# Feed forward of a decoder layer: down projection by token with seven quadrant products in place of eight

## The chip, the cores and the metric

One core of one Trainium2 chip. The metric is the time on the device of one execution, in microseconds (us), and lower is better. The engines are TensorE (PE; its weight loads are listed as PEld), VectorE (DVE), ScalarE (ACT), GpSimd (POOL) and SyncE (SP, which issues the kernel's loads). L12 means line 12 of the kernel before.

## What is computed

A decoder layer on 512 tokens of 1024 features in float32. The part around the change:

```
h   = layer_norm(alpha * h + mixed @ w_out, ln1_g, ln1_b)
mlp = square(relu(h @ w_up)) @ w_down        # 1024 -> 4096 -> 1024
r   = alpha * h + mlp
ple = sigmoid(r @ ple_gate_w) * (p @ ple_proj_w)
h   = layer_norm(r + ple, ln2_g, ln2_b)
```

Ahead of it stand an input norm, a combined input projection, a gated delta rule, a pooling mixer and their merge; these the change leaves as they are.

## The kernel before

Wide products run as three passes in float32r over a split of both operands into a high part with 12 significant bits and the rest: high times high, high times low, low times high (`three`, L65). A weight slab of 512 KB is loaded by SP into one of three raw buffers, copied by ACT into the high part and subtracted by DVE into the low part (`load`, L50 to L59; four buffers each for high and low). The activations `act` are kept by feature: [feature, token], in eight blocks of 128 features, each with a high and a low half (L47).

The work goes in stages: the mixers, the output projection `ps_wo` with the norm LN1 (`out_done`, L790), the projection `ps_pp` of p, and from L824 on the feed forward, the gate product and LN2. LN1 normalises 128 tokens at a time in place in `y`, transposes them on PE and writes them to `act` with gain and offset (`to_features`, L109).

The feed forward runs twice over half of the 4096 hidden features (`fh`, L836). Each half makes 8 up slabs of 256 features; per block of 128 features PE runs 24 matmuls of 128x512 (weights held still, tokens moving), ACT takes relu and square (L846, L848), DVE squares again and subtracts for the low part (L849, L850). The 16 blocks of hidden activations stay in the buffers `hid`. Then come the 8 output blocks of the down projection, 96 matmuls each (L860), in two banks at a time; the first half adds alpha times `act` and stores to `rp` (L865, L867), the second adds `rp` (L870), splits into `act` (L871, L872), transposes with four small matmuls per block (L875) and copies back to `rp` (L876), so that r is there by feature for the gate and by token for the residual.

The gate product (`tok_gemm`, L745, called at L918) holds tokens still and moves weights: first 512 columns for all four token blocks with the features outermost, then the other 512 columns block by block, the last in two pieces. `ple_done` (L880) applies the sigmoid on ACT, multiplies by `pproj` on DVE (L886) and adds `rp`, on POOL for the first 512 columns and on DVE for the rest (L887); with the last columns of a block come the statistics and LN2, shared out to DVE, ACT and POOL by `plan` (L895), and the output is stored.

Nothing of the order is written out by hand here: a scheduler places instructions by their order in the program, priorities (`tc.high_priority`) and simulated times; `tc.issue_after` puts instructions behind another one on its engine. Each engine and each queue then runs its list in order. PSUM has eight banks of [128, 512]: six of tag `g` and two of tag `tp` in this stage.

## Time and profile before

| | |
|---|---|
| time, median of 3 runs | 887.84 us (886.15 to 889.31) |
| the profiled execution | span 886.5 us; no other time is listed for it |
| granted clock of PE, mean | 0.990 |
| up and down projections, first up matmul to last down matmul | 476.5 to 829 us |
| first down matmul | 564.7 us |
| last matmul of the gate product | starts at 873.63 us |
| HBM | 77.74 MB read, 90 GB/s over the span |

Busy time is per engine, from the start to the end of each instruction. PE's matmuls overlap: the duration of one is not the distance to the next. "Idle before" is an engine's idle time ahead of a group, followed by what ended it; it costs something only where the engine is the one that sets the time. The DMA row names the issuing queue, the number of issues, the size and the median time from issue to landing. The rows that matter are shown in the prediction.

### The profile page before, as it was taken

What the parts mean: (1) busy time and instruction counts of PE and PEld (TensorE: products, weight loads), DVE (VectorE), ACT (ScalarE), POOL (GpSimd) and SP (SyncE); (2) the same over time, 40 slices, a digit from 0 to 9 for tenths busy, and PEclk for the clock granted to TensorE, in tenths of its full rate; (3) what the DMA queues carried; (4) which work ended last, traced back from release to release, by engine and by line L of the source; (5) the groups of instructions that cost most, each with busy time, mean ns of one, the idle gap of its engine ahead of it and who ended that gap; (6) DMA issues with size and microseconds to landing.
All of it is one profiled execution on the core that took longest, in us unless ns stands there. A gap on an engine that the chain in (4) does not pass through costs nothing.

```text
span 886.5 us, 12477 instructions
## 1 busy us (share of the span) xinstructions
PE 860.3 (97%) x4944; PEld 715.3 (81%) x4944; DVE 521.7 (59%) x991; ACT 357.5 (40%) x567; POOL 151.6 (17%) x135
## 2 busy tenths in 40 slices
PE   7999999999999999998999999999999999999994
PEld 5777888888888888886888888888888888888883
DVE  8898988769759336368366544433344443333456
ACT  4566455365544535333136444322124442222311
POOL 6182312113403031324000000000000000000034
PEclk9999999999999999999999999999999999999997
DMA  6322222222211313183215333333323323233202
GB/s 196 96 59 85 72 73 80 65 72 72 78 50 53 97 31 97 52 283 96 72 32 182 96 95 95 119 96 95 95 85 103 99 95 96 95 96 95 95 10 86
DMA packets 72427, 80.63 MB, mean 91 GB/s; under 512 B 4009, under 2 KB 64818, under 8 KB 72370
## 3 DMA queue, kind: packets, MB, share of 16 engines
q1 hardware_dynamic: 72370, 79.85, 29.6%
q8 instruction: 39, 0.64, 0.3%
q14 instruction: 18, 0.15, 0.1%
HBM read 77.74 MB, written 2.10 MB: 90 GB/s over the span
## 4 chain that ended last, share of the span: by engine, by line
PE 89%; DVE 6%; ACT 2%; POOL 1%; issue 1%; DMA 1%; SPq 0%; POOLq 0%; ACTq 0%; DVEq 0%
PE ps_dn L67 7%; PE ps_dn L68 7%; PE ps_dn L66 7%; PE ps_up L67 6%; PE ps_up L68 6%; PE ps_up L66 6%; PE ps_z L67 2%; PE ps_z L68 2%; PE ps_gb L66 2%; PE ps_gb L68 2%; PE ps_v L67 2%; PE ps_z L66 2%; PE ps_gb L67 2%; PE ps_v L68 2%; PE ps_v L66 2%; PE ps_ga L66 2%
## 5 line engine op out<-in xcount | busy, mean ns | idle before, releaser
L67 PE MATMUL ps_dn<-hid,hi_dn 128*128 128x512 f32 x256 | 99.9, 390 | 0.0
L68 PE MATMUL ps_dn<-hid,lo_dn 128*128 128x512 f32 x256 | 99.9, 390 | 0.0
L66 PE MATMUL ps_dn<-hid,hi_dn 128*128 128x512 f32 x256 | 99.7, 389 | 0.0
L58 DVE TENSOR_TENSOR lo_dn<-raw_dn,hi_dn 128x1024 fp32r<-128x1024 f32 x32 | 39.2, 1225 | 82.9 <-ACT hi_dn L57 82.9
L57 ACT CAST hi_dn<-raw_dn 128x1024 fp32r<-128x1024 f32 x32 | 33.7, 1054 | 96.8 <-PE ps_dn L67 85.2
L887 POOL TENSOR_TENSOR y<-y,rp 128x512 f32<-128x512 f32 x4 | 6.3, 1613 | 380.5 <-PE ps_pg L756 380.5
L66 PEld LDWEIGHTS ps_dn<-hid,hi_dn 128*128 128x128 f32 x256 | 48.1, 188 | 10.0
L67 PEld LDWEIGHTS ps_dn<-hid,hi_dn 128*128 128x128 f32 x256 | 48.1, 188 | 10.0
L68 PEld LDWEIGHTS ps_dn<-hid,lo_dn 128*128 128x128 f32 x256 | 48.1, 188 | 9.7
L849 DVE TENSOR_TENSOR relu<-relu 128x512 f32<-128x512 f32 x32 | 22.2, 693 | 53.3 <-ACT hid L848 53.3
L846 ACT ACTIVATE relu<-ps_up 128x512 f32<-128x512 f32 x32 | 19.0, 595 | 55.8 <-PE ps_up L68 55.8
L693 POOL TENSOR_TENSOR zs<-zs,sgb 128x512 f32<-128x512 f32 x8 | 15.0, 1875 | 88.0 <-ACT sgb L692 88.0
L850 DVE TENSOR_TENSOR hid<-relu,hid 128x512 fp32r<-128x512 f32 x32 | 22.1, 691 | 1.1
L352 DVE SCALAR_TENSOR_TENSOR acc_q<-ps_q,ccol,acc_q 128x511 f32<-128x511 f32 (+2 forms) x24 | 17.8, 742 | 6.3 <-ACT acc_q L350 6.0
L848 ACT ACTIVATE hid<-relu 128x512 fp32r<-128x512 f32 x32 | 20.3, 633 | 1.0
L451 DVE TENSOR_TENSOR sh<-sh,ya 128x120 f32<-128x120 f32 (+14 forms) x60 | 19.4, 324 | 0.7
L356 POOL TENSOR_TENSOR kq<-acc_k,sg_k 128x512 f32<-128x512 f32 x8 | 10.9, 1366 | 48.9 <-ACT sg_k L355 48.9
L58 DVE TENSOR_TENSOR lo_pg<-raw_pg,hi_pg 128x1024 fp32r<-128x1024 f32 x8 | 9.6, 1222 | 16.3 <-ACT hi_pg L57 16.3
L121 ACT ACTIVATE hf_l<-ps_l,pcol 128x128 f32<-128x128 f32 x32 | 11.9, 472 | 17.1 <-PE ps_l L116 17.1
L557 ACT ACTIVATE vn<-ps_s,cc 128x128 f32<-128x128 f32 x32 | 11.1, 367 | 18.6 <-PE ps_s L555 18.5
L352 DVE SCALAR_TENSOR_TENSOR acc_k<-ps_k,ccol,acc_k 128x511 f32<-128x511 f32 (+2 forms) x24 | 17.8, 742 | 1.3 <-ACT acc_k L350 1.2
L58 DVE TENSOR_TENSOR lo_wo<-raw_wo,hi_wo 128x1024 fp32r<-128x1024 f32 x8 | 10.8, 1354 | 13.0 <-ACT hi_wo L57 13.0
(947 smaller groups left out, 2557.0 us busy)
## 6 DMA issues: line engine op xcount, KB each, us to landing
raw_dn<-in_w_down_dram SPq DMA_DIRECT2D x32, 512.0 KB, 3.5
raw_wo<-in_w_out_dram SPq DMA_DIRECT2D x8, 512.0 KB, 4.0
raw_pg<-in_ple_gate_w_dram SPq DMA_DIRECT2D x8, 512.0 KB, 3.6
x<-in_x_dram SPq DMA_DIRECT2D x8, 256.0 KB, 5.3
y<-in_x_dram SPq DMA_DIRECT2D x4, 512.0 KB, 9.3
out_dram<-y SPq DMA_DIRECT2D x7, 256.0 KB, 2.0
raw_k<-in_w_in_dram SPq DMA_DIRECT2D x2, 512.0 KB, 4.0
raw_pp<-in_ple_proj_w_dram SPq DMA_DIRECT2D x2, 512.0 KB
```

Of the source, the lines that this page charges most:

```text
L57: A.copy(hi, raw)
L58: V.tensor_tensor(out=lo, in0=raw, in1=hi.bitcast(F32), op=SUB)
L66: T.matmul(ps, wh, ah, start=first, stop=False)
L67: T.matmul(ps, wh, al, start=False, stop=False)
L68: T.matmul(ps, wl, ah, start=False, stop=last)
L352: marks[name + "v"] = V.scalar_tensor_tensor(out=acc[:, s:], in0=ps[:, :SEQ - s], scalar=w(3 - s), in1=acc[:, s:], op0=MULT, op1=ADD)
L451: V.tensor_tensor(out=sh[:, :, :m], in0=sh[:, :, :m], in1=ya[:, :, k:k + 1].to_broadcast([P, U8, m]), op=MULT)
L693: G.tensor_tensor(out=zs[m], in0=zs[m], in1=sg, op=MULT)
L846: A.activation(r, ps, AF.Relu)
L848: A.activation(hl[:, 0, :], r, AF.Square)
L849: V.tensor_tensor(out=r, in0=r, in1=r, op=MULT)
L850: V.tensor_tensor(out=hl[:, 1, :], in0=r, in1=hl[:, 0, :].bitcast(F32), op=SUB)
```

## The change

The down projection is computed by token, [token, feature], in eight chunks `c` of 512 hidden features, and each chunk's product is made by Strassen's scheme (in Winograd's form). The activations are cut into two halves of tokens (rows) and, within each block of 256 features `j`, two blocks of 128 features (the inner halves); `w_down` into the matching inner halves and two halves of 512 columns. Seven products take the place of eight.

- The left operands are made on DVE. After relu and square (both on ACT now, into `r2`), the quarters a11 (`ha`) and a12, a22 (`hb`) are split for products 1, 2 and 4; four subtractions of [128, 256] make the sums in place in `r2`, and these are split into `hs` for products 6, 7, 3 and 5.
- The right operands are sums of weight quarters, made by DMA. SP loads four quarters of 512 KB a chunk into buffers of their own (`dx`, six). POOL adds other quarters onto them with accumulating DMAs, two of 256 KB per quarter: one sum onto `y`, and three in turn onto `x`. Between the sums on `x` its value is split (`halves`) for the next product: 1, then 5, then 6, then 4. The split parts have buffers of their own (`dhi`, `dlo`, four each).
- The results. Products 1 and 6 gather in four banks of their own over all chunks (`perm`, tag `u`). Products 2, 5 and 7 go into the banks of tag `g` (now four) and are added by DVE to the residual `res` in each chunk (`gather`); products 3 and 4 are made on top of 5 and 7 in the same banks and added too. In the last chunk the standing banks are added as well.
- The residual is kept by token: LN1 writes its normalised rows to `res` in a pool of its own, and in the first chunk DVE applies LN1's gain and offset to it, times alpha, with eight operations of [128, 1024].
- r is transposed for the gate by `features`, per block of 128 tokens. The gate product goes by tokens: all 1024 columns of a block, then the next. DVE makes all additions; POOL none. All eight gate slabs are loaded and split ahead, four of them into `dhi` and `dlo`.
- The up slabs of later chunks have a smaller priority offset (40 in place of 300) and are put behind the splits of the chunk before.

The core of the diff (the feed forward before, removed as a whole, is in the listing above):

```diff
-    def load(src, c, name, keep=None, tags=("whi", "wlo"), nb=4):
...
-        with tc.high_priority(offset=300):
+        with tc.high_priority(offset=ahead):
...
+    rsp = root.enter_context(tc.tile_pool(name="rsp", bufs=1, side="right"))
...
+    res = [rsp.tile([P, DM], F32, name=f"res_{t}") for t in range(NT)]
...
-            V.tensor_scalar(out=y, in0=y, scalar1=mv[:, 0:1], scalar2=rstd, op0=SUB, op1=MULT)
-            to_features(y, t, g_1, b_1, pp2, ("tp",), 2, tpa, "l1")
+            V.tensor_scalar(out=res[t], in0=y, scalar1=mv[:, 0:1], scalar2=rstd, op0=SUB, op1=MULT)
+            to_features(res[t], t, g_1, b_1, pp2, ("tp",), 2, tpa, "l1")
...
+    def g3(name):
+        return pp3.tile([P, SEQ], F32, tag="g", bufs=4, name=name)
+    perm = {i: [pp3.tile([P, SEQ], F32, tag="u", bufs=4, name=f"ps_dn{i}_{m}") for m in range(2)]
+            for i in (1, 6)}
+    NC = 8
+    DXB = 6
+    gb1 = tp3.tile([P, 2, DM], F32, tag="hs", bufs=2, name="gb1")
+    dma(out=gb1[:, 0, :], in_=ln1_g[0].partition_broadcast(P))
+    dma(out=gb1[:, 1, :], in_=ln1_b[0].partition_broadcast(P))
+    def quarter(c, i, half):
+        src = w_down[0, 512 * c:512 * c + 512, 512 * half:512 * half + 512]
+        return src.rearrange("(j i p) n -> i p j n", i=2, p=P)[i]
+    def chain(c, name, i, half):
+        raw = tp3.tile([P, 2, 512], F32, tag="dx", bufs=DXB, name=f"{name}_{c}")
+        dma(out=raw, in_=quarter(c, i, half))
+        return raw
+    def onto_chain(raw, c, i, half):
+        for j in range(2):
+            G.dma_start(out=raw[:, j, :], in_=quarter(c, i, half)[:, j, :], accum_op=ADD)
+    def halves(raw, name):
+        hi = tp3.tile([P, 2, 512], F32R, tag="dhi", bufs=4, name=f"hi_{name}")
+        lo = tp3.tile([P, 2, 512], F32R, tag="dlo", bufs=4, name=f"lo_{name}")
+        marks["dn"] = (A.copy(hi, raw), V.tensor_tensor(out=lo, in0=raw, in1=hi.bitcast(F32), op=SUB))
+        return hi, lo
+    def hidden(c):
+        left = []
+        for j in range(2):
+            c0 = 512 * c + 256 * j
+            with ExitStack() as queue:
+                for ins in behind[j]:
+                    queue.enter_context(tc.issue_after(ins.ins))
+                gr = [slab(w_up[0], k0, c0, f"up{c}{j}{k0}", ahead=40 if c else 300) for k0 in (0, 512)]
+            r2 = tp3.tile([P, 2, SEQ], F32, tag="r2", bufs=2, name=f"r2_{c}{j}")
+            ha = tp3.tile([P, 2, HT], F32R, tag="ha", bufs=2, name=f"hid_a{c}{j}")
+            hb = tp3.tile([P, 2, SEQ], F32R, tag="hb", bufs=2, name=f"hid_b{c}{j}")
+            hs = tp3.tile([P, 2, 2, SEQ], F32R, tag="hs", bufs=2, name=f"hid_s{c}{j}")
+            for i in range(2):
+                ps = g3(f"ps_up{c}{j}{i}")
+                gemm_tile(ps, gr, i, HALVES if c == 0 and j == 0 else ((0, SEQ),))
+                A.activation(r2[:, i, :], ps, AF.Relu)
+                A.activation(r2[:, i, :], r2[:, i, :], AF.Square)
+                src, dst = (r2[:, 1, :], hb) if i else (r2[:, 0, 0:HT], ha)
+                A.copy(dst[:, 0, :], src)
+                V.tensor_tensor(out=dst[:, 1, :], in0=src, in1=dst[:, 0, :].bitcast(F32), op=SUB)
+            a11, a21, a12, a22 = r2[:, 0, 0:HT], r2[:, 0, HT:], r2[:, 1, 0:HT], r2[:, 1, HT:]
+            V.tensor_tensor(out=a22, in0=a21, in1=a22, op=SUB)
+            V.tensor_tensor(out=a21, in0=a11, in1=a21, op=SUB)
+            V.tensor_tensor(out=a11, in0=a11, in1=a22, op=SUB)
+            V.tensor_tensor(out=a12, in0=a12, in1=a11, op=SUB)
+            for k in (1, 0):
+                act_last = A.copy(hs[:, 0, k, :], r2[:, k, :])
+                vec_last = V.tensor_tensor(out=hs[:, 1, k, :], in0=r2[:, k, :], in1=hs[:, 0, k, :].bitcast(F32),
+                                           op=SUB)
+            at = {1: (lambda q, h=ha: h[:, q, :]), 2: (lambda q, h=hb: h[:, q, 0:HT]),
+                  4: (lambda q, h=hb: h[:, q, HT:])}
+            for k, i in enumerate((6, 7, 3, 5)):
+                at[i] = lambda q, h=hs[:, :, k // 2, HT * (k % 2):HT * (k % 2) + HT]: h[:, q, :]
+            left.append(at)
+        behind[0] = (act_last, vec_last)
+        return left
+    def product(i, left, right, banks, first, last, pairs=(0, 1), onto=False):
+        hi, lo = right
+        for j in pairs:
+            for m in range(2):
+                ms = slice(m * P, (m + 1) * P)
+                ah, al = left[j][i](0)[:, ms], left[j][i](1)[:, ms]
+                f, l = first and j == 0, last and j == 1
+                T.matmul(banks[m], ah, hi[:, j, :], start=f, stop=False, skip_group_check=onto)
+                T.matmul(banks[m], ah, lo[:, j, :], start=False, stop=False, skip_group_check=onto)
+                done = T.matmul(banks[m], al, hi[:, j, :], start=False, stop=l, skip_group_check=onto)
+        return done
+    behind = [(), ()]
+    def gather(banks, row, half, op=ADD):
+        for m in range(2):
+            dst = res[2 * row + m][:, 512 * half:512 * half + 512]
+            if op == ADD:
+                V.tensor_tensor(out=dst, in0=banks[m], in1=dst, op=ADD)
+            else:
+                V.tensor_tensor(out=dst, in0=dst, in1=banks[m], op=SUB)
+    def features(t):
+        for half in range(2):
+            ps = pp3.tile([P, 4, P], F32, tag="u", bufs=4, name=f"ps_rt{t}{half}")
+            for a in range(4):
+                kb = 4 * half + a
+                T.transpose(ps[:, a, :], res[t][:, kb * P:(kb + 1) * P], ident)
+            ks, ts = slice(4 * half, 4 * half + 4), slice(t * P, (t + 1) * P)
+            A.copy(act[:, ks, 0, ts], ps)
+            V.tensor_tensor(out=act[:, ks, 1, ts], in0=ps, in1=act[:, ks, 0, ts].bitcast(F32), op=SUB)
+    def start_chains(c):
+        x, z, y = chain(c, "x", 0, 0), chain(c, "z", 1, 0), chain(c, "y", 0, 1)
+        onto_chain(y, c, 1, 1)
+        return x, z, y, chain(c, "w", 1, 1)
+    chains = start_chains(0)
+    for c in range(NC):
+        fst, lst = c == 0, c == NC - 1
+        x, z, y, b22 = chains
+        w = {1: halves(x, f"dn{c}_1")}
+        onto_chain(x, c, 0, 1)
+        w[2] = halves(z, f"dn{c}_2")
+        w[5] = halves(x, f"dn{c}_5")
+        onto_chain(x, c, 1, 1)
+        left = hidden(c)
+        w[6] = halves(x, f"dn{c}_6")
+        onto_chain(x, c, 1, 0)
+        if fst:
+            for t in range(NT):
+                V.scalar_tensor_tensor(out=res[t], in0=res[t], scalar=ALPHA, in1=gb1[:, 0, :], op0=MULT, op1=MULT)
+                V.scalar_tensor_tensor(out=res[t], in0=gb1[:, 1, :], scalar=ALPHA, in1=res[t], op0=MULT, op1=ADD)
+        if not lst:
+            chains = start_chains(c + 1)
+        zb = [g3(f"ps_dnz_{c}{m}") for m in range(2)]
+        xb = [g3(f"ps_dnx_{c}{m}") for m in range(2)]
+        yb = [g3(f"ps_dny_{c}{m}") for m in range(2)]
+        p1 = lambda pairs: product(1, left, w[1], perm[1], fst, lst, pairs)
+        p2 = lambda pairs: product(2, left, w[2], zb, True, True, pairs)
+        p5 = lambda: product(5, left, w[5], xb, True, True)
+        p6 = lambda: product(6, left, w[6], perm[6], fst, lst)
+        p7 = lambda: product(7, left, w[7], yb, True, True)
+        if not lst:
+            p1((0,)), p2((0,)), p1((1,)), p2((1,))
+            gather(zb, 0, 0)
+            w[7] = halves(y, f"dn{c}_7")
+            p5()
+            gather(xb, 1, 1)
+            w[3] = halves(b22, f"dn{c}_3")
+            behind[1] = marks["dn"]
+            p6()
+            w[4] = halves(x, f"dn{c}_4")
+            p7()
+            gather(yb, 1, 1, SUB)
+            product(3, left, w[3], xb, False, True, onto=True)
+            gather(xb, 0, 1)
+            product(4, left, w[4], yb, False, True, onto=True)
+            gather(yb, 1, 0)
+            continue
+        p1((0,)), p2((0,)), p1((1,)), p2((1,))
+        gather(zb, 0, 0)
+        w[3] = halves(b22, f"dn{c}_3")
+        p5()
+        gather(perm[1], 0, 0)
+        gather(xb, 1, 1)
+        w[7] = halves(y, f"dn{c}_7")
+        us, u2 = [], tp3.tile([P, 2, SEQ], F32, tag="r2", bufs=2, name="u")
+        for m in range(2):
+            A.copy(u2[:, m, :], perm[1][m])
+            us.append(u2[:, m, :])
+        p6()
+        for m in range(2):
+            V.tensor_tensor(out=us[m], in0=perm[6][m], in1=us[m], op=SUB)
+        gather(us, 0, 1)
+        w[4] = halves(x, f"dn{c}_4")
+        product(3, left, w[3], xb, False, True, onto=True)
+        gather(xb, 0, 1)
+        p7()
+        features(0)
+        gather(us, 1, 1)
+        gather(yb, 1, 1, SUB)
+        features(1)
+        product(4, left, w[4], yb, False, True, onto=True)
+        gather(us, 1, 0, SUB)
+        gather(yb, 1, 0)
+    features(2)
+    features(3)
...
+    gates = []
+    for half in range(2):
+        kw = dict(keep=tp3, tags=("dhi", "dlo")) if half else {}
+        gates.append([rslab(ple_gate_w[0], 256 * i, 512 * half, f"pg{half}{i}", **kw) for i in range(4)])
+    for t in range(NT):
+        cuts = (0, 512, 1024) if t < NT - 1 else (0, 512, 768, 1024)
+        st = tp3.tile([P, 3, 6], F32, tag="st", bufs=2, name=f"st_l2{t}")
+        for n, (c0, c1) in enumerate(zip(cuts, cuts[1:])):
+            half, w0, w1 = c0 // 512, c0 % 512, (c1 - 1) % 512 + 1
+            ps = pp3.tile([P, SEQ], F32, tag="g", bufs=4, name=f"ps_pg{t}{n}")[:, 0:c1 - c0]
+            for kb in range(KB):
+                hi, lo = gates[half][kb // 2]
+                ah, al = (act[:, kb, q, t * P:(t + 1) * P] for q in range(2))
+                T.matmul(ps, ah, hi[:, kb % 2, w0:w1], start=kb == 0, stop=False)
+                T.matmul(ps, ah, lo[:, kb % 2, w0:w1], start=False, stop=False)
+                T.matmul(ps, al, hi[:, kb % 2, w0:w1], start=False, stop=kb == KB - 1)
+            sg = tp3.tile([P, SEQ], F32, tag="r2", bufs=2, name=f"sg_{t}{n}")[:, 0:c1 - c0]
+            A.activation(sg, ps, AF.Sigmoid)
+            V.tensor_tensor(out=sg, in0=sg, in1=pproj[t, half][:, w0:w1], op=MULT)
+            y = res[t][:, c0:c1]
+            V.tensor_tensor(out=y, in0=y, in1=sg, op=ADD)
+            V.bn_stats(out=st[:, n, :], in_=y)
...
+        plan = (((0, 512, "V"), (512, 1024, "G")), ((0, 512, "V"), (512, 1024, "G")),
...
```

79 lines of the change are left out of this document (10 added, 69 removed).

## The prediction

> **What bounds the kernel now.** I read the page's head first, then busy time by stretches, then single matmuls in order of time, and last who waits for whom.
>
> ```profile
> span 886.5 us, 12477 instructions
> PE 860.3 (97%) x4944; PEld 715.3 (81%) x4944; DVE 521.7 (59%) x991; ACT 357.5 (40%) x567; POOL 151.6 (17%) x135
> ```
>
> ```profile
> 476.00:831.00 355.00, 354.66 (x1625) 295.52 (x1624) 145.63 (x165) 117.99 (x153) 0.00 (x0) 1.00 0.33 100
> 831.00:874.00 43.00, 42.91 (x216) 36.33 (x214) 25.95 (x36) 9.64 (x15) 12.22 (x10) 1.00 0.11 39
> 874.00:887.00 13.00, 0.00 (x0) 0.00 (x0) 7.86 (x14) 1.59 (x3) 6.18 (x6) 0.57 0.21 81
> ```
>
> The columns of the stretches are: length; busy time of PE, PEld, DVE, ACT and POOL; granted clock; DMA share; GB/s. The first row is the feed forward (up and down), the second the rest of the gate product, the third the tail. PE is busy in 354.66 of 355.00 us at clock 1.00, while DVE is busy in 41% and ACT in 33% of it, and POOL does nothing. So in the stage that changes, time is the number of matmuls times their spacing. The spacing is not the duration that the groups show:
>
> ```profile
> 599.82 0.39 PE L67 MATMUL ps_dn<-hid,hi_dn 128*128 128x512 f32 x1
> ...
> 603.90 0.39 PE L67 MATMUL ps_dn<-hid,hi_dn 128*128 128x512 f32 x1
> ```
>
> Columns: start, duration, instruction. A matmul of 128x512 lasts 0.39 us, but they start much closer: from 599.82 to 603.90 there are 18 steps, so the pitch is 4.08 / 18 = 0.2267 us. Whoever multiplied by the 0.39 would see a gain 1.7 times too big.
>
> The tail is a second bound: the last matmul starts at 873.63 and the span ends 12.9 us later.
>
> **The matmuls.** Before, the down projection has 3 x 256 = 768 matmuls (256 for each of L66, L67, L68, group below). After, each of 8 chunks of 512 hidden features makes seven products; each is 2 feature pairs x 2 blocks of 128 tokens x 3 passes = 12 matmuls of 128x512. That is 8 x 84 = 672, so 96 fewer. The up projection keeps its count; the 32 transposes of r stay 32; the gate product keeps its matmuls too. The three passes now hold tokens still and move weights, as the output projection and the gate product already do; loads per matmul stay at one. Gain: 96 x 0.2267 = **21.8 us**. A chunk then takes (96 + 84) x 0.2267 = 40.8 us on PE: 21.8 for up, 19.0 for the products.
>
> **DVE and ACT per chunk.**
>
> ```profile
> L67 PE MATMUL ps_dn<-hid,hi_dn 128*128 128x512 f32 x256 | 99.9, 390 | 0.0
> L58 DVE TENSOR_TENSOR lo_dn<-raw_dn,hi_dn 128x1024 fp32r<-128x1024 f32 x32 | 39.2, 1225 | 82.9 <-ACT hi_dn L57 82.9
> L57 ACT CAST hi_dn<-raw_dn 128x1024 fp32r<-128x1024 f32 x32 | 33.7, 1054 | 96.8 <-PE ps_dn L67 85.2 <-PE ps_up L67 11.6
> L848 ACT ACTIVATE hid<-relu 128x512 fp32r<-128x512 f32 x32 | 20.3, 633 | 1.0
> L846 ACT ACTIVATE relu<-ps_up 128x512 f32<-128x512 f32 x32 | 19.0, 595 | 55.8 <-PE ps_up L68 55.8
> L870 DVE TENSOR_TENSOR rp<-ps_dn,rp 128x512 f32<-128x512 f32 x8 | 5.5, 690 | 3.8 <-PE ps_dn L68 3.8
> L871 ACT CAST act<-rp 128x512 fp32r<-128x512 f32 x8 | 4.9, 618 | 9.9 <-DVE rp L870 9.9
> L703 DVE TENSOR_TENSOR lo_lift<-raw_lift,hi_lift 128x256 fp32r<-128x256 f32 x2 | 0.8, 416 | 0.0
> ```
>
> DVE: 11 weight splits (4 up, 7 down) x 1.225 = 13.5; per block of 256 features 5 half-width subtractions x 0.416 and 3 full ones x 0.69 = 4.2, twice 8.3; ten additions of a bank into the residual x 0.69 = 6.9. Together 28.7 of 40.8 us (70%; before 41%). ACT: 11 x 1.054 = 11.6; relu 4 x 0.595 = 2.4; square 4 x 0.633 = 2.5; copies about 4.5 by the 0.618 row. Together 21.0 (51%). Neither exceeds PE, so as totals they cost nothing; what costs is the order at the hand-offs.
>
> Count from the end of a chunk's up part. The products start at 0 (1 and 2, first pair), 2.7 (second pair), 5.4 (product 5), 8.2 (6), 10.9 (7), 13.6 (3), 16.3 (4). Product 2's second pair, at 4.1, needs relu, square, copy and subtraction of the last up tile: 0.6 + 0.63 + 0.62 + 0.69 = 2.5, so 1.6 us are spare. Product 5's second pair, at 6.8, needs on top four sums (1.7), a copy and a subtraction (1.3): 5.5, so 1.3 spare. One weight split ahead in a queue takes 1.05 on ACT or 1.22 on DVE, so most times the slack just holds; two in a row (2.3) do not. In the 19.0 us of the products DVE must do 3.75 for the second block, 8 additions (5.5) and 6 splits (7.35): 16.6, that is 87%. Bounds for both hand-offs together: 0 and 2 us a chunk. I take 0.5, since each slack exceeds one queued split: **+3.5** over the first seven chunks.
>
> **The accumulating DMAs.** Four 512 KB quarters per chunk are added onto others by 8 DMAs from POOL. The trace has no DMA of that queue and none that accumulates:
>
> ```profile
> q1 hardware_dynamic: 72370, 79.85, 29.6%
> ...
> raw_dn<-in_w_down_dram SPq DMA_DIRECT2D x32, 512.0 KB, 3.5
> ...
> y<-in_x_dram SPq DMA_DIRECT2D x4, 512.0 KB, 9.3
> ```
>
> Call A the time from a split's end until the next sum of 512 KB has landed. Lower bound: 3.5, the same bytes loaded plainly in the same stage. Upper bound: twice the slowest 512 KB row, 18.6, since an added byte is also read back from its destination. I take 7, twice the row of the same source and stage. [...]
>
> In the steady state the chain is: split for 6, product 6 (2.7), split for 1 of the next chunk, A, split for 5, A, split for 6. A split is 1.05 + 1.22 = 2.3, so it returns every 9.6 + 2A us. At A = 7 that is 23.6 of 40.8: hidden, and it binds only from A = 15.6. A sum that comes late stands in ACT's queue as a waiting copy; behind it stand the next chunk's relus, whose banks PE needs again only at the products. On POOL only other accumulations stand behind a waiting one. On SP the load of y waits until the split for 4 frees x's buffer (about 11 us into the products); behind it stand w and the next up slabs, needed 8 us later, which covers a landing of 3.5. Traffic rises from 100 GB/s, at which the first stretch has the DMA engines busy for 0.33, to 6.3 MB in 40.8 us, 154 GB/s, or about half; I add nothing for it.
>
> **The first chunk.**
>
> ```profile
> 476.52 0.36 PE L66 MATMUL ps_up<-act,hi_up00a 128*128 128x256 f32 x1
> ...
> 478.68 0.50 SPq L828 DMA_DIRECT2D gb<-in_ln_g_dram  x1
> ```
>
> The first load of this stage's own pool was issued at 478.68, and I put x there. Landed at 483 and split by 485.3, it is ready for product 4 at 485.3 + 3A + 3 x 2.3 = 513.2 for A = 7. PE ends the first up part at 476.5 + 21.8 + 0.3 = 498.6 and wants product 4 at 514.9. So A = 7 just fits, and each us above 7.6 costs 3. The residual's gain and offset add 8 operations of 128x1024:
>
> ```profile
> L670 DVE TENSOR_TENSOR y<-y,gb_in 128x1024 f32<-128x1024 f32 x4 | 7.1, 1764 | 0.0
> L671 DVE TENSOR_TENSOR y<-y,gb_in 128x1024 f32<-128x1024 f32 x4 | 4.8, 1213 | 0.0
> ```
>
> That is 9.7 to 14.1 us of DVE inside the first up part, beside four splits (4.9) and the first block's 4.2; and the second block's sums wait for gb1's buffer. Cost 0 to 4; **+1.5**.
>
> **The last chunk and the gate.** Before the gate can start, DVE does 3.75 for the block, 14 additions and subtractions of banks (9.7), 3 splits (3.7) and 2 subtractions for the first 128 tokens (1.4): 18.6 in 19.0 + 0.9 us of PE work, with PE's products 3, 7 and 4 waiting in between for single ones. All 20 bank operations, 8 feature subtractions and 4 gate splits ahead of the gate would make 31.7. Cost 0 to 12; I take **+3.5**, because the gate's first 22 us need two token blocks only and cover the rest.
>
> **The tail.**
>
> ```profile
> 864.12 0.69 DVE L887 TENSOR_TENSOR y<-y,rp 128x512 f32<-128x512 f32 x1
> ...
> 870.27 1.62 POOL L912 TENSOR_TENSOR y<-y,gb 128x512 f32<-128x512 f32 x1
> ...
> 870.77 1.67 DVE L887 TENSOR_TENSOR y<-y,rp 128x512 f32<-128x512 f32 x1
> ...
> 873.32 0.37 DVE L886 TENSOR_TENSOR y<-y,pproj 128x256 f32<-128x256 f32 x1
> ...
> 873.63 0.28 PE L770 MATMUL ps_pg<-hi_pg,act 128*128 128x256 f32 x1
> ...
> 876.50 0.36 ACT L884 ACTIVATE y<-ps_pg 128x256 f32<-128x256 f32 x1
> ...
> 879.65 0.43 DVE L780 BATCH_NORM_STATS2 st_l<-y 128x6 f32<-128x256 f32 x1
> ```
>
> The last tokens' sigmoid starts 2.6 us after PE's end because ACT and DVE still work on the tokens before, and two DVE operations beside POOL's take up to 1.67 instead of 0.69. From PE's end (873.9) to the end of the last statistics (880.1) it is 6.2 us. After the change the gate goes by tokens: 48 matmuls, 10.9 us, lie between one block's end and the next, and DVE's share of a block (six operations of 0.69, and the norm) is well under that, so the last 256 columns find free engines: 0.36 + 0.37 + 0.42 (the 0.416 row) + 0.43 and gaps, about 2.0. What follows the statistics stays. **-4.2** (bounds -4.5 and 0).
>
> **Sum:** 886.5 - 21.8 - 4.2 + 3.5 + 1.5 + 3.5 = 869.0 in the profile's span. The page gives no other time for that execution; the median of the three runs, 887.84, lies 1.3 above it, so I forecast **870**.
>
> **The rivals.** Full gain: none of the three costs appears, 887.84 - 26.0 = 861.8. For it: every hand-off has slack. Against it: DVE at 87% in the products.
>
> Hand-offs lose: two splits ahead in a queue at one hand-off and one at the other cost about 2 us in each chunk, 16 in all, with 6 in the last chunk and 1.5 in the first: 861.8 + 23.5 = 885.3, no measurable change. POOL's issues could bring it about: if each stretched one DVE operation by the 0.98 us that L887 shows (1.67 against 0.69), DVE would gain 8 us a chunk, 36.7 of 40.8, and 90 to 100% in the products. [...]
>
> Slow accumulation (slower): the forecast's lead of 17.5 us over the median is gone when the first chunk waits 3 x (A - 7.6) = 17.5, so from A = 13.4. At A = 16 the first chunk waits 25 us and seven later periods 0.8 each: 870 + 25 + 6 = 901; at 18.6, 33 + 42 make 945. For it: nothing in the trace has run this way, and 9.3 exists for a plain load. Against it: 3.5 in this very stage.
>
> **How the numbers follow.** Forecast 0.50 (864 to 878), full gain 0.20, hand-offs lose 0.16 (878 to 890), slow accumulation 0.14. A measurement of this kernel tells about 0.3% (2.7 us) from no change. Faster: 0.50 + 0.20 + two thirds of 0.16 = 0.81; same: 0.05; slower: 0.14. Of the full gain a quarter may fall below 861 and of the rest 0.15 above 888, so 861 to 888 holds 8 in 10; the forecast case alone spans 864 to 878.
>
> **What would show it.** Right: the same pitch of 0.227 in the products, 672 of them, about 41 us from one chunk's first up matmul to the next, idle PE in the feed forward below 10 us in total, and the last statistics about 2 us behind the last matmul. The accumulation row, issue to landing, near 3 to 4 us for each 256 KB half would confirm A. Wrong: PE idle before product 5, 6 or 4 with a DMA as its releaser behind ACT's copy (slow accumulation); PE idle in every chunk before product 2 or 5, released by DVE (hand-offs); a long gap between the last product and the first gate matmul (last chunk too cheap).

## The result and the profile after

The changed kernel takes 917.55 us (median of 4 runs, 914.24 to 921.58), the kernel before 887.31 us on the same chip (886.15 to 889.31). The ratio is 1.0335 (95% interval 1.0302 to 1.0369): slower by 30 us where 870 had been forecast, and outside the range. The profiled execution of after is the fastest of its four (914.24 us); the others, at a mean granted clock of 0.964 to 0.973 instead of 0.976, took 917.18 to 921.58. In what follows L numbers of the changed kernel are its own (`product` is at L926 to L928, `gather` at L937 and L939).

The head of the page of the kernel after, and three stretches of it (columns as in the prediction):

```profile
span 912.5 us, 12688 instructions
PE 854.6 (94%) x4848; PEld 705.0 (77%) x4848; DVE 614.8 (67%) x1155; ACT 406.6 (45%) x650; POOL 208.8 (23%) x198
```

```profile
476.00:857.00 381.00, 345.20 (x1503) 281.61 (x1501) 238.66 (x323) 166.37 (x234) 57.02 (x64) 0.96 0.57 141
857.00:903.40 46.40, 46.25 (x237) 39.34 (x235) 31.48 (x44) 10.48 (x18) 14.15 (x12) 1.00 0.09 35
903.40:912.50 9.10, 0.00 (x0) 0.00 (x0) 4.48 (x11) 0.78 (x2) 1.95 (x2) 0.66 0.17 59
```

The 96 matmuls are gone (4944 to 4848), yet the span is 26 us longer. PE, before busy in 354.66 of 355.00 us of the feed forward, now stands idle for 36 us of the first stretch, at a mean granted clock of 0.96 instead of 1.00. What it waits for is in the list of PE's waits (columns: us in total, times, longest):

```profile
PE ps_dnx L926 <- DVE res L937: 17.1, 6, 3.1
PE ps_rt L947 <- DVE res L937: 6.7, 1, 6.7
PE ps_dn L926 <- ACT hid_a L897: 3.8, 1, 3.8
PE ps_dn L926 <- ACT hi_dn L874: 3.3, 1, 3.3
```

The first row returns in six of the first seven chunks: product 3 (banks `ps_dnx`) waits until DVE has added those banks, as product 5 left them, to the residual. In the one left over, the third, the same place has a wait of 2.89 us that the profile puts to ACT (`hi_dn`). The other three rows are one event each: the second in the last chunk, the third and fourth in the first.

It helps to cut the feed forward at each chunk's first up matmul: 475.99, 534.73, 579.30, 624.02, 668.62, 714.09, 759.56, 806.25. A chunk without a wait would take 40.8 us. The first took 58.7. Of the 17.9 above 40.8, 1.3 are not new: in both kernels the first 96 up matmuls are half as wide (128x256) and take 12.2 us where 48 of 128x512 take 10.9. So the first chunk lost 16.6. The six that follow took 44.6 to 46.7, 45.25 on average (6 x 4.45 = +26.7). From the last chunk's first up matmul to the last matmul, 902.98, it is 96.7 us; in the kernel before the same way is 873.63 - 476.52 - 7 x 43.52 = 92.5, less 2.7 for 12 matmuls and less the 1.3 that belong to the first chunk, so 88.4 was to be had (+8.3). The tail, from the start of the last matmul to the end, went from 12.9 to 9.5 (-3.4). With -21.8 for the matmuls and -0.5 for an earlier start that is 25.9 of the 26.0 us.

Look at one hand-off of the second chunk, PE in order of time, and what DVE did meanwhile:

```profile
569.41 0.39 PE L928 MATMUL ps_dny<-hi_dn,hid_s 128*128 128x512 f32 x1
569.64 0.61 PE L928 MATMUL ps_dnx<-hi_dn,hid_s 128*128 128x512 f32 x2
573.04 0.47 PE L926 MATMUL ps_dnx<-hi_dn,hid_s 128*128 128x512 f32 x1 [2.79 <-DVE res L937]
```

```profile
567.07 0.68 DVE L907 TENSOR_TENSOR hid_s<-r,hid_s 128x512 fp32r<-128x512 f32 x1
567.67 1.22 DVE L874 TENSOR_TENSOR lo_dn<-w,hi_dn 128x1024 fp32r<-128x1024 f32 x1
568.80 1.22 DVE L58 TENSOR_TENSOR lo_up<-raw_up,hi_up 128x1024 fp32r<-128x1024 f32 x1
569.94 1.21 DVE L874 TENSOR_TENSOR lo_dn<-x,hi_dn 128x1024 fp32r<-128x1024 f32 x1
571.07 1.22 DVE L58 TENSOR_TENSOR lo_up<-raw_up,hi_up 128x1024 fp32r<-128x1024 f32 x1
572.21 1.28 DVE L937 TENSOR_TENSOR res<-ps_dnx,res 128x512 f32<-128x512 f32 x2
```

The products do not run in the order of the program. The first row ends product 7 (`ps_dny`); the second is the last pass of product 5, two matmuls put behind product 7 when the order was built; the third is product 3, which accumulates onto the same banks. So product 5's additions cannot start before 570.25, and product 3 can start only behind them. On DVE a split is running by then, another stands ahead of the additions, and the first addition itself takes about 0.7. Together that is 2.79 us of idle PE.

### The profile page after: what moved, and what is told of

It is laid out like the page before. It is cut to its first block, busy times and chain, and to the rows that moved or that the text cites. A ratio compares the mean times of both kernels' runs of the same rounds, so it can differ in the third digit from the quotient of the medians.

```text
span 912.5 us, 12688 instructions
## 1 busy us (share of the span) xinstructions
PE 854.6 (94%) x4848; PEld 705.0 (77%) x4848; DVE 614.8 (67%) x1155; ACT 406.6 (45%) x650; POOL 208.8 (23%) x198
## 3 DMA queue, kind: packets, MB, share of 16 engines
q0 software_dynamic: 9216, 16.78, 11.6%
## 4 chain that ended last, share of the span: by engine, by line
PE 71%; DVE 15%; issue 5%; DMA 3%; ACT 2%; POOL 2%; SPq 0%; POOLq 0%; DVEq 0%; ACTq 0%
PE ps_up L68 6%; PE ps_up L66 6%; PE ps_up L67 6%; DVE lo_dn L874 3%; PE ps_z L67 2%; PE ps_z L68 2%; PE ps_gb L66 2%; PE ps_gb L68 2%; PE ps_z L66 2%; PE ps_gb L67 2%; DVE lo_up L58 2%; DVE res L937 2%; PE ps_q L66 1%; PE ps_q L68 1%; PE ps_q L67 1%
## 5 line engine op out<-in xcount | busy, mean ns | idle before, releaser
L67 PE MATMUL ps_up<-act,hi_up 128*128 128x512 f32 (+1 forms) x272 | 102.5, 377 | 0.3 <-DVE act L124 0.3
L66 PE MATMUL ps_up<-act,hi_up 128*128 128x512 f32 (+1 forms) x272 | 102.5, 377 | 0.0
L68 PE MATMUL ps_up<-act,lo_up 128*128 128x512 f32 (+1 forms) x272 | 102.4, 376 | 0.0
L874 DVE TENSOR_TENSOR lo_dn<-x,hi_dn 128x1024 fp32r<-128x1024 f32 x32 | 39.0, 1219 | 92.8 <-ACT hi_dn L874 92.8
L874 ACT CAST hi_dn<-x 128x1024 fp32r<-128x1024 f32 x32 | 33.4, 1048 | 146.8 <-DMA x<-in_w_down_dram 146.4
L869 POOL DMA_DIRECT2D x<-in_w_down_dram x48 | 43.0, 1069 | 229.7 <-DVE lo_dn L874 220.4
L67 PEld LDWEIGHTS ps_up<-act,hi_up 128*128 128x128 f32 x272 | 51.2, 188 | 9.9 <-DVE act L124 0.5
L68 PEld LDWEIGHTS ps_up<-act,lo_up 128*128 128x128 f32 x272 | 51.2, 188 | 9.4
L66 PEld LDWEIGHTS ps_up<-act,hi_up 128*128 128x128 f32 x272 | 51.2, 188 | 9.3
L926 PE MATMUL ps_dnx<-hi_dn,hid_s 128*128 128x512 f32 x64 | 28.6, 447 | 19.9 <-DVE res L937 17.1
L58 DVE TENSOR_TENSOR lo_up<-raw_up,hi_up 128x1024 fp32r<-128x1024 f32 x32 | 38.8, 1216 | 2.0 <-ACT hi_up L57 2.0
L696 POOL TENSOR_TENSOR zs<-zs,sgb 128x512 f32<-128x512 f32 x8 | 17.9, 2244 | 90.9 <-ACT sgb L695 90.9
L926 PEld LDWEIGHTS ps_dnx<-hi_dn,hid_s 128*128 128x128 f32 x64 | 13.8, 215 | 25.6 <-ACT hi_dn L874 19.2
L906 ACT CAST hid_s<-r 128x512 fp32r<-128x512 f32 x32 | 19.1, 617 | 18.9 <-DVE r L903 17.8
L1049 PE MATMUL ps_pg<-hi_pg,act 128*128 128x512 f32 (+1 forms) x72 | 27.0, 375 | 0.0
L928 PE MATMUL ps_dnx<-hi_dn,hid_s 128*128 128x512 f32 x64 | 26.9, 440 | 0.0
L1051 PE MATMUL ps_pg<-hi_pg,act 128*128 128x512 f32 (+1 forms) x72 | 26.6, 369 | 0.0
```

The source lines that it names most:

```text
L58: V.tensor_tensor(out=lo, in0=raw, in1=hi.bitcast(F32), op=SUB)
L66: T.matmul(ps, wh, ah, start=first, stop=False)
L67: T.matmul(ps, wh, al, start=False, stop=False)
L68: T.matmul(ps, wl, ah, start=False, stop=last)
L869: G.dma_start(out=raw[:, j, :], in_=quarter(c, i, half)[:, j, :], accum_op=ADD)
L874: marks["dn"] = (A.copy(hi, raw), V.tensor_tensor(out=lo, in0=raw, in1=hi.bitcast(F32), op=SUB))
```

## The experiments

Two theories went in. A: the order of the queues costs the time. B: the new accumulating DMAs cost it. All ratios are to the kernel before on the same chip. "Steady" is the mean of the chunks between the first and the last.

**Without the sums** (the accumulating DMAs are left out, so the weight sums are missing from four of the seven products, 4 to 7):

```diff
-            G.dma_start(out=raw[:, j, :], in_=quarter(c, i, half)[:, j, :], accum_op=ADD)
+            pass
```

> This kernel leaves out the accumulating DMAs, so the weight sums are missing from the products. Theory A (order on VectorE): from the second chunk on, the time is lost because the additions of product 5 stand behind weight splits in VectorE's queue, with no DMA in it; so the period of chunks 2 to 7 stays at 44 to 47 us, and only the first chunk, whose chain of sums the trace shows late, gets shorter, from 58.7 to about 46 us. In all 903 to 908 us. Theory B (the accumulating DMAs are the cost, through late sums and through traffic that delays the other loads): the period falls to 41 us too, and the time to about 875 us.

Measured: 901.77 us, 1.0176 (1.0132 to 1.0221). First chunk 48.1 us instead of 58.7, steady 45.0 instead of 45.25. That is theory A's picture, and the time lies a little below its 903 to 908. PE's waits:

```profile
PE ps_dnx L926 <- DVE res L937: 20.4, 7, 3.7
PE ps_rt L947 <- DVE res L937: 6.8, 1, 6.8
```

Both rows of DVE are still there without a single sum. So the steady part owes the DMAs at most 0.2 us a chunk and the last chunk nothing (106.1 us to the end of the span, against 106.3); the first chunk owes them 10.6 us.

**Plain copies in place of the sums** (the same bytes overwrite instead of being added, so the weight sums are missing):

```diff
-            G.dma_start(out=raw[:, j, :], in_=quarter(c, i, half)[:, j, :], accum_op=ADD)
+            G.dma_start(out=raw[:, j, :], in_=quarter(c, i, half)[:, j, :])
```

> The same DMAs from GpSimd with the same bytes and waits, but each overwrites instead of adding, so the products get single quarters. If the addition is what makes a sum take 8 to 9 us, a step of the chain falls to about 4 us (a plain load of this size), the first chunk by about 12 us, and the time to about 905 us. If the queue, the descriptors and the traffic make it, a step stays at 8 us and the time within 3 us of 917. Theory A (order on VectorE) expects the chunks 2 to 7 at 44 to 47 us either way.

Measured: 907.84 us, 1.0234 (1.0215 to 1.0253); first chunk 52.4, steady 45.0. The first chunk gained half of the 12 us expected. The DMA rows of after, then of this run:

```profile
q0 software_dynamic: 9216, 16.78, 11.6%
...
x<-in_w_down_dram POOLq DMA_DIRECT2D x48, 256.0 KB, 5.5
```

```profile
q0 software_dynamic: 5120, 16.78, 5.3%
...
x<-in_w_down_dram POOLq DMA_DIRECT2D x48, 256.0 KB, 3.6
```

For the same 16.78 MB the adding form takes 9216 packets instead of 5120 and about twice the DMA engines' time, and a half lands 5.5 us after its issue instead of 3.6. Of the first chunk's 10.6 us, 6.4 are the adding and 4.2 the copying.

**Product 5's additions ahead of the splits, on DVE alone** (and product 7's ahead of the next chunk's first two splits):

```diff
+            first_add = gather(xb, 1, 1)
...
+            with tc.issue_after(first_add.ins):
+                w[4] = halves(x, f"dn{c}_4")
...
+            adds[c] = gather(yb, 1, 1, SUB)
...
+            behind[0] = behind[0] + (first_add,)
+            behind[1] = (marks["dn"][0], last_add)
```

> Only the order on VectorE changes in chunks 1 to 7: product 5's additions go ahead of the split for product 4 and of the next up slabs' splits, product 7's ahead of the next chunk's splits for 1 and 2. Theory A: the 2.8 us of idle PE ahead of product 3 are gone, the granted clock behind it stays at 1.00, the period is 41 to 42 us, and the time falls by 20 to 27 us to 890 to 898. Theory B (the accumulating DMAs): no change, 914 to 921 us. Theory C (the clock falls through the load of all engines, not through PE's idle time): the idle time goes, the slow pitch of 0.43 us in product 3 stays, 900 to 905 us.

Measured: 908.87 us, 1.0231 (1.0201 to 1.0262); steady 44.6. A miss: the wait ahead of product 3 fell from 2.8 to 0.7 us and returned ahead of product 4, 11.3 us over seven chunks, since product 7's additions now stood behind three splits. DVE itself waited 1.84 us for product 5's last pass, which is how its late place on PE came to light. On that run's theory C, that load lowers the clock, the traces speak as well: with as much work on DVE and ACT, but no wait of PE above 1.63 us, the mean granted clock from the second chunk to the last (532.4 to 800 us) was 1.00, in after (534.7 to 806.2) 0.97. So, as far as these runs show, the drop goes with PE's idle time and not with the load.

**The first chunk's loads:** x and z ahead of the gains and of the second chunk's up slabs, x's sum ahead of y's, the residual's operations behind x's first split.

```diff
-        x, z, y = chain(c, "x", 0, 0), chain(c, "z", 1, 0), chain(c, "y", 0, 1)
+        x, z = chain(c, "x", 0, 0), chain(c, "z", 1, 0)
+        if c == 0:
+            dma(out=gb1[:, 0, :], in_=ln1_g[0].partition_broadcast(P))
...
+            with tc.issue_after(lo_first.ins):
+                for t in range(NT):
```

> Only the first chunk's chain changes: the loads of x and z are issued ahead of LN1's gain and of the second chunk's up slabs, y's sum goes behind x's first sum on GpSimd, and the eight operations on the residual stand behind x's first split on VectorE. If the late chain (x landed 486.7 us, its first split ended 4 us later, three sums of 8 to 9 us) causes the first chunk's 18 us, the chain starts 8 to 12 us earlier and the first chunk takes 45 to 50 us instead of 58.7: 906 to 912 us in all, with chunks 2 to 7 unchanged. If the first chunk is lost to something else, for example the four waiting banks or the second block's operands, less than 3 us come back: 914 us or more.

Measured: 906.47 us, 1.0216 (1.0196 to 1.0237); first chunk 50.0 instead of 58.7. So 8.8 of that chunk's 16.6 us came from where its loads, sums and first split stood.

**The products in program order on PE, alone:**

```diff
-            p1((0,)), p2((0,)), p1((1,)), p2((1,))
+            done = p2((0,), p1((0,)))
+            done = p2((1,), p1((1,), done))
...
+            done = p5(done)
```

> The seven products of a chunk keep their own order on TensorE (each product's matmuls behind the last one of the product before), in all chunks but the last; nothing else differs, and VectorE's order is left to itself. In the changed kernel the last two matmuls of product 5 stand behind product 7, directly ahead of product 3, which accumulates onto the same banks. Theory A (that place is what makes product 3 wait for the additions of product 5): the wait ahead of product 3, 2.8 us a chunk, falls to 1 us or less, the clock no longer drops there, and a chunk of the steady part takes 41 to 43 us instead of 44.6 to 46.7, so 895 to 902 us in all against 917.5. Rival B (VectorE itself is too full while the products run, whatever their order): the wait moves to product 4, to the eviction of product 2 or to the next chunk's relus, a chunk still takes 44 us or more, and the time is 910 to 918 us. The first chunk (58.7 us) and the last one stay as they are under both.

Measured: 923.55 us, 1.0408 (1.0378 to 1.0439); first chunk 63.2, steady 46.8. Slower than after, and outside both theories' numbers. PE's waits:

```profile
PE ps_dnx L930 <- ACT hid_s L906: 12.1, 7, 3.9
PE ps_dnx L932 <- DVE hid_s L907: 11.2, 6, 2.0
```

The wait for the additions is gone and two others stand in its place: product 5's second pair now meets operands (`hid_s`) that ACT and DVE have not made yet. The odd order of after had covered that. So late `hid_s` looks like the deeper cause; the runs with `hid_s` early, below, test it.

**Both orders:** that of PE, and on DVE the additions of products 5, 7 and 3 ahead of the splits that can wait (product 3's weights, the next chunk's up slabs and first down slabs).

```diff
+            xb_read = gather(xb, 1, 1)
+            with tc.issue_after(xb_read.ins):
+                w[3] = halves(b22, f"dn{c}_3")
...
+            yb_read = gather(yb, 1, 1, SUB)
...
+            behind[0] = behind[0] + (xb_read,)
+            second[0] = (yb_read,)
+            behind[1] = (marks["dn"][0], adds[c])
```

> The order of the products on TensorE as in the run before, and on VectorE as well: the additions that read product 5's banks stand ahead of the split of product 3's weights, the next chunk's first up slabs are split behind the additions of products 5 and 7, and its second slabs and first down slabs behind the additions of product 3. Theory A (order alone costs the steady part its 4 us a chunk): each product finds its banks read and its weights split, a chunk takes 41 to 41.8 us, that is 890 to 898 us in all. Rival B (VectorE has more work in the products than they last): a chunk takes 43 us or more, with the wait at product 4 or at the next chunk's up projection, 905 us or more.

Measured: 913.08 us, 1.0279 (1.0245 to 1.0313); steady 43.95, first chunk 61.3. By these numbers rival B holds, but not in its place: of all waits in the steady part only ACT's `hid_s` is left, 1.4 to 2.2 us a chunk, and none for product 4's banks or the next up tiles.

**The last chunk alone:** the second row's additions and five gate splits behind the first tokens' residual (`row0`).

```diff
+        with tc.issue_after(row0.ins):
+            gather(us, 1, 1)
...
+            with tc.issue_after(row0.ins) if half or i > 1 else nullcontext():
+                gates[half].append(rslab(ple_gate_w[0], 256 * i, 512 * half, f"pg{half}{i}", **kw))
```

> Only the last chunk differs from the changed kernel: the second row's additions and five of the eight gate splits stand on VectorE behind the residual of the first tokens. If the 6.7 us that TensorE waits ahead of the transposes of the last part is VectorE's queue in that place, that wait falls to 1 to 2 us and the time by 5 to 8 us, to 910 to 913 us. If it only moves to the gate's matmuls, which then wait for their splits, the time falls by less than 2 us.

Measured: 907.5 us, 1.0233 (1.019 to 1.0275), 2.5 us below the expected range; the way from the last chunk's first up matmul to the end of the span went from 106.3 to 99.7 us, and the wait ahead of the transposes from 6.7 to 0.9. So DVE's queue in that place was nearly all of that wait. Some 3.5 of the 10 us lie elsewhere and are not explained.

**All three stages:** both orders, the first chunk's loads and the last chunk, their three edits together. Of the lines at which they meet:

```diff
+                    for ins in behind[j] + (second[0] if k0 and j == 0 else ()) + ((loads[3],) if c == 1 else ()):
```

> The orders of the run before, and the two ends as well: in the first chunk the loads of the first down weights are issued ahead of the second chunk's up slabs and the residual's operations stand behind the first split, in the last chunk the second row's additions and five gate splits stand behind the first tokens' residual. Theory A (the steady part's 4 us a chunk, the first chunk's 9 us and the last one's 3 to 6 us are all order, and they add): 872 to 885 us, less than the 887 us of the kernel before. Rival B (what is freed at one place is lost at the next, since VectorE's work stays the same): 890 us or more.

Measured: 893.33 us (9 runs), 1.0073 (1.0051 to 1.0096): 24 us back. By the number that is rival B (890 or more), but what is freed at one place is not lost at the next: both orders, the first chunk and the last chunk had alone given 4.5, 11.1 and 10.1 us, about as much in sum. Theory A's range was missed in the steady chunks. First chunk 49.8, steady 43.3, with 1.4 to 2.1 us of waiting for `hid_s` in each.

**`hid_s` early, in two steps.** First, on top of all three stages, both casts of `hid_s` ahead of the next chunk's up slabs on ACT, and their low parts ahead of product 2's additions on DVE:

```diff
-        behind[0] = (act_last, vec_last)
+        behind[0] = lasts
...
+            with after_all(*mark[1]):
+                gather(zb, 0, 0)
+                w[7] = halves(y, f"dn{c}_7")
```

> As the run with all three stages, and only the second step of the run beside it: both casts of hid_s ahead of the next chunk's up slabs on ScalarE, their low parts ahead of product 2's additions on VectorE. Product 6's copy keeps its place in ScalarE's queue, ahead of the relus. If that copy makes the relus late (theory A), product 5 still waits 1 us or more a chunk here and the time is 886 to 892 us; if it is the order behind the relus (rival B), the wait goes here too and the time is that of the other run but for the first chunk, 878 to 884 us.

Second, that and product 6's weight copy, which waits for its sum, behind the relu and the cast of the second pair's first up tile; in the first chunk the gains ahead of z and product 5's copy ahead of the second pair's relus:

```diff
+        with after_all(*mark["ab", 1, 1 if fst else 0]):
+            w[6] = halves(x, f"dn{c}_6")
```

> On top of the orders of the run with all three stages: on ScalarE product 6's weight copy, which waits for its sum, stands behind the relu and the cast of the second pair's first up tile, and both casts of hid_s stand ahead of the next chunk's up slabs; on VectorE their low parts stand ahead of product 2's additions; in the first chunk the residual's gains are loaded ahead of z, and product 5's weight copy stands ahead of the second pair's relus. In the run before, product 5's second pair still waited 1.4 to 2.1 us a chunk for hid_s, and ScalarE stood up to 5.7 us at product 6's copy with the relus behind it. Theory A (the prediction's claim that such a late copy harms nobody was wrong: the relus behind it make the wait): product 5's wait goes, a steady chunk takes 40.8 to 41.2 us, the first one 45 to 48 us, and the whole 872 to 880 us, under the 887 us of the kernel before. Rival B (VectorE's queue makes hid_s late, not the relus): the wait stays over 1 us and the time over 885 us.

Measured: 878.81 us, 0.9899 (0.9881 to 0.9917) for the first step alone, steady 41.25; **871.2 us, 0.9795 (0.9772 to 0.9818)** for both, steady 40.80. So the late casts and low parts of `hid_s` cost about 2.1 us a chunk, and the copy that waits for its sum 0.45 and 4.4 in the last chunk. Of the first step's two theories that is rival B: the order behind the relus, more than the copy, made `hid_s` late in the steady chunks. The second step's edits of the first chunk brought nothing (48.4 and 48.5 us, where 45 to 48 were expected). This kernel beats both others. Its head, and the first up matmuls of its second and its last chunk:

```profile
span 869.5 us, 12694 instructions
PE 841.1 (97%) x4848; PEld 698.2 (80%) x4848; DVE 615.5 (71%) x1155; ACT 408.8 (47%) x650; POOL 205.3 (24%) x198
```

```profile
524.96 0.39 PE L66 MATMUL ps_up<-act,hi_up 128*128 128x512 f32 x1
...
769.76 0.39 PE L66 MATMUL ps_up<-act,hi_up 128*128 128x512 f32 x1
```

Six chunks lie between: 244.8 / 6 = 40.8 us each, what 180 matmuls at the pitch of 0.2267 need.

**The two steps on the kernel after, without any prescribed order of products or of the additions of products 5, 7 and 3:**

```diff
-        behind[0] = (act_last, vec_last)
+        behind[0] = lasts
...
+        with after_all(*mark["ab", 1, 1 if fst else 0]):
+            w[6] = halves(x, f"dn{c}_6")
...
+            with after_all(*mark[1]):
+                gather(zb, 0, 0)
+                w[7] = halves(y, f"dn{c}_7")
```

> Only the queues around the second pair's relus differ from the changed kernel: product 6's weight copy stands behind that pair's first relu and cast on ScalarE, both casts of hid_s ahead of the next chunk's up slabs, their low parts ahead of product 2's additions. No order of the products on TensorE and none of product 5's additions is prescribed, but with hid_s early the build itself sets product 5's last pass ahead of product 7. Theory A (the copy that waits for its sum is the root of the steady part's loss, and the late place of product 5's last pass only followed from it): a chunk of the steady part takes 41 to 42 us, the wait ahead of product 3 is under 1 us, and the time falls from 917.5 to 893 to 900 us; the first and the last chunk keep their losses. Rival B (VectorE's splits ahead of the additions are a second cause of their own): product 3 still waits 1 to 2 us, a chunk takes 43 to 44 us and the time is 903 to 912 us.

Measured: 901.96 us, 1.0149 (1.0127 to 1.017); steady 43.5. As expected the build now puts product 5's last pass ahead of product 7, and the wait ahead of product 3 is gone; but PE waits twice in each chunk for additions that stand behind splits on DVE:

```profile
PE ps_dny L928 <- DVE res L949: 9.1, 8, 1.2
PE ps_up L66 <- DVE res L947: 6.9, 6, 1.2
```

Late `hid_s` is the cause of the odd order on PE, and the order on DVE is a second cause of its own. That is rival B by its mechanism and its 43 to 44 us a chunk, though the wait moved from product 3 to product 4 and the next up tile, and the time lies a little below B's 903 to 912.

**The best kernel without the sums** (missing from products 4 to 7, as in the first experiment):

```diff
-            sums.append(G.dma_start(out=raw[:, j, :], in_=quarter(c, i, half)[:, j, :], accum_op=ADD))
+            pass
```

> The best kernel so far (871 us) without its accumulating DMAs, so that the weight sums are missing from five of the seven products; the chain of casts stays. Its steady chunks already take 40.8 us, what 180 matmuls need. Theory A (ordered, the sums are hidden in all chunks but the first): 868 to 871 us, with the saving, 1 to 3 us, in the first chunk alone. Rival B (the sums still cost somewhere, by DMA traffic or by the clock): 866 us or less.

Measured: 862.6 us, 0.9716 (0.9694 to 0.9738); first chunk 42.15 us, steady 40.80 again. By its number that is rival B, and it shows where: the sums cost nothing in the steady chunks; in the first one they still cost 6.3 us, more than the 1 to 3 of theory A, and about 1 us behind the last chunk's first up matmul.

## Why the prediction was wrong

**The matmuls: right.** The pitch in the products is 0.2267 us where nothing waits, and the best kernel's steady chunk is 40.80 us to the digit. All versions have 4848 matmuls, and the best kernel shows the 21.8 us.

**DVE and ACT per chunk: right as totals.** In 244.7 us of the best kernel's six steady chunks DVE is busy for 163.11 and ACT for 119.64 us:

```profile
525.00:769.70 244.70, 244.70 (x1081) 202.64 (x1080) 163.11 (x223) 119.64 (x162) 42.55 (x49) 1.00 0.61 151
```

That is 27.2 and 19.9 a chunk, against 28.7 and 21.0 predicted, with 151 GB/s against 154. PE is busy in all of it. POOL's issues, which the prediction feared, stretched nothing visible: a weight split on DVE took 1.22 us on average in after, as before.

**The hand-offs: the step that failed.** Of the 43.5 us between the span forecast, 869.0, and the one measured, 912.5, 23.2 are here, 15.1 in the first chunk, 4.8 in the last one and 0.8 in the tail, less 0.5 for an earlier start. The prediction said: "I take 0.5, since each slack exceeds one queued split: +3.5". The six chunks in the middle alone lost 26.7 us. Three things were wrong. The list of hand-offs ended with product 5's second pair; the one that cost most, product 3 onto the banks of product 5 behind DVE's additions, is not on it, nor is product 4 onto those of product 7. The start times assumed the order of the program on PE, while the order is set at build, and product 5's last pass ran some 5 us later; with `hid_s` early the build put it back ahead of product 7. And DVE was given 6 splits in the products; in after it has 9 there (the weights of products 7, 3 and 4, the next chunk's for products 1 and 2, and four up slabs), and more than one stands ahead of the additions. The rival "hand-offs lose" had the kind of mechanism, two splits ahead in a queue, and 2 us a chunk, but not the place, and less than half the price.

**The clock adds to it.** In the six chunks PE's idle time makes 18.3 of the 26.7 us; the other 8.4 are matmuls that followed a wait and started further apart. After the same idle of 2.79 us some chunks went on at full pitch and some not:

```profile
800.57 0.63 PE L926 MATMUL ps_dnx<-hi_dn,hid_s 128*128 128x512 f32 x1
801.00 0.63 PE L927 MATMUL ps_dnx<-lo_dn,hid_s 128*128 128x512 f32 x1
...
803.98 0.39 PE L928 MATMUL ps_dny<-hi_dn,hid_b 128*128 128x512 f32 x1
804.21 0.39 PE L926 MATMUL ps_dny<-hi_dn,hid_b 128*128 128x512 f32 x1
```

```profile
564.00:579.00 15.00, 11.76 (x51) 9.16 (x50) 14.83 (x18) 6.55 (x8) 1.77 (x2) 1.00 0.90 268
797.80:806.20 8.40, 8.33 (x24) 6.65 (x25) 5.97 (x8) 0.27 (x1) 1.77 (x2) 0.63 0.62 128
```

Around the wait that ended at 573.04 the granted clock stayed 1.00; behind the one that ended at 797.87 it was 0.63 on average, and matmuls started 0.43 us apart instead of 0.2267 until 803.98; in these 6.1 us alone the granted clock was 0.50. Likewise it was 0.50 from 708.38 to 711.77 and 0.51 from 752.70 to 756.06. That makes the periods 45.5, 45.5 and 46.7 where others are 44.6. What sets these three chunks apart from those that stayed at 1.00 after an idle of 2.8 to 2.9 us is not shown.

**The late copy: wrong in the argument.** "A sum that comes late stands in ACT's queue as a waiting copy; behind it stand the next chunk's relus, whose banks PE needs again only at the products." The relus did stand behind it:

```profile
591.71 1.05 ACT L874 CAST hi_dn<-x 128x1024 fp32r<-128x1024 f32 x1 [5.50 <-DMA x<-in_w_down_dram]
592.66 0.40 ACT L897 CAST hid_a<-r 128x256 fp32r<-128x256 f32 x1
592.97 0.60 ACT L894 ACTIVATE r<-ps_up 128x512 f32<-128x512 f32 x1
```

This relu's up tile (second of the chunk that began at 579.30, 48 matmuls) ended near 590.2; with the copy moved, the same relu of the best kernel came 0.2 us behind its tile. It is not the banks that matter but the relu's result, which product 5 needs. Price, measured with the other orders set: 0.45 us a steady chunk and 4.4 in the last one, 7.6 us of the whole time; in the first chunk of after it passed the late sum on to PE (below).

**The accumulating DMAs: A too small in the first chunk, the bound right.** In the first chunk of after it took 9.0 us from the first split's end to the next sum's arrival, then about 8, above the 7 taken; for the third chunk's sums it took 8.5 and 6.3. All lie inside the bounds of 3.5 to 18.6. In the steady state that binds nothing, as the limit of 15.6 said and the run without sums shows. One half alone took 5.5 us from issue to landing with the addition and 3.6 without, where the prediction looked for 3 to 4 us with it. The rival "slow accumulation" with a loss over the forecast's lead did not come: without any sums the kernel was still 1.0176 times as long as before. (That lead is 887.84 - 870 = 17.8, not 17.5; the rival's condition hardly moves.)

**The first chunk: +1.5 predicted, +16.6 measured.** x was issued at 479.16, about as assumed, but landed 7.6 us later instead of 4.3, and its split waited for the residual:

```profile
483.94 4.63 DVE L972 SCALAR_TENSOR_TENSOR res<-res,gb 128x1024 f32<-128x1024 f32 x4 [3.02 <-DMA gb<-in_ln_g_dram]
488.49 3.49 DVE L973 SCALAR_TENSOR_TENSOR res<-gb,res 128x1024 f32<-128x1024 f32 x3
491.90 1.22 DVE L874 TENSOR_TENSOR lo_dn<-x,hi_dn 128x1024 fp32r<-128x1024 f32 x1
```

So the chain began at 493.1 instead of 485.3, 7.8 us late, and the three sums took some 4 us more than 3 x 7. PE met this not at product 4, as the prediction had it, but earlier:

```profile
502.17 1.04 ACT L874 CAST hi_dn<-x 128x1024 fp32r<-128x1024 f32 x1 [10.10 <-DMA x<-in_w_down_dram]
503.12 0.59 ACT L894 ACTIVATE r<-ps_up 128x512 f32<-128x512 f32 x1
505.76 0.50 PE L926 MATMUL ps_dn<-hi_dn,hid_a 128*128 128x512 f32 x1 [3.79 <-ACT hid_a L897]
513.50 0.96 PE L926 MATMUL ps_dn<-hi_dn,hid_s 128*128 128x512 f32 x2 [3.26 <-ACT hi_dn L874]
```

The copy that waits for the first sum holds up the relu of an up tile that PE had ended near 493.6, and with it product 1's second pair; then product 6 waits for the copy of the second sum. Neither wait is in the run without sums, whose first chunk was 10.6 us shorter; the other 6.0 us were there without any sum, 3.7 of them the wait ahead of product 3. The prediction counted the eight operations as DVE time and not as a queue ahead of the split. With loads and split first the loss was 7.9, in the best kernel 6.4, and there without sums nothing: the eight operations, put in that order, cost none of the 1.5 taken for them.

**The last chunk: +3.5 predicted, +8.3 measured,** inside the bounds of 0 to 12. Its mechanism was right (DVE's additions and gate splits ahead of the first 128 tokens), its cover was not: "the gate's first 22 us need two token blocks only" says nothing for the first block. In the best kernel it is +1.7.

**The tail: right but for 0.8 us.** The last statistics end 2.1 us behind the start of the last matmul (2.0 predicted); what follows them took 7.4 instead of 6.4 us, so -3.4 instead of -4.2.

The forecast of 869.0 for the span is close to the best kernel's 869.5, partly by chance: hand-offs 0 instead of 3.5, last chunk 1.7 instead of 3.5, first chunk 6.4 instead of 1.5, tail -3.3 instead of -4.2. It was a forecast of what the change can give, not of the order in which it was given. Whether PE's prescribed order is needed once `hid_s` and the additions are early was not tried.

## What to carry to other kernels

List as hand-offs not only the operands of each product but its banks: here product 3, which accumulates onto banks that DVE must read first, waited up to 3.1 us a chunk for what stood ahead of that reading in DVE's queue. Where a scheduler builds the order, take start times from no order that it does not guarantee, and ask what makes an operand late before forcing an order: PE's order forced alone made the kernel slower, while with operands and additions early and both ends put in order as well it was 5% faster than after. A saving of 2.5% in an engine that was busy all the time was lost here to a wait of about 3 us in every round and the slower matmuls behind it, and two late ends.

## What the runs showed of the hardware

An idle of 2.79 us on PE was followed in some chunks by about 3 to 6 us of matmuls at 0.43 us distance and a granted clock of 0.50 to 0.51, in others by none, with the same instructions around it; in the run with product 5's additions first, no wait of the steady chunks was longer than 1.63 us and none was followed by that distance. An accumulating DMA of 256 KB took 5.5 us from issue to landing where a plain one from the same queue took 3.6, with 9216 packets instead of 5120 and 11.6% instead of 5.3% of the DMA engines' time for 16.78 MB.
